# First state-space scan of a hybrid diffusion step: three task lists spread differently over the scan's steps

## The chip, the cores and the metric

The kernel runs on one core of a Trainium2 chip. A core has five engines that run their own instruction queues side by side: TensorE (PE in the rows: matrix products), VectorE (DVE: elementwise work), ScalarE (ACT: copies and activations), GpSimd (POOL, hardly used here) and SyncE (SP), whose queue issues most of the DMA transfers between HBM and the core's memory. Each queue is worked in order: an instruction that waits holds up all that stand behind it on its engine. The metric is the device time of one execution in microseconds (us), lower is better; the median of several runs is compared.

## What is computed

One inference step of a four-layer backbone on 128 context and 256 latent tokens, width 1024. Layers 0 and 3 are bidirectional diagonal state-space (S5) mixers, layer 1 pools, layer 2 is latent attention. Cut to what matters for layer 0:

```python
sh, sc, g = split(silu(cond) @ ada_w[layer] + ada_b[layer], 3)     # "conditioning", for every layer
h = rmsnorm(x) * (1 + sc) + sh
u, z = split(h @ w_in, 2)                                           # 2048 columns each
for dirn in (0, 1):                                                 # forward and backward
    bu = einsum('blgc,gpc->blgp', u_grouped, b_bar)
    states = scan(s[t] = lam_bar * s[t-1] + bu[t])                  # complex, diagonal
    y = y + real(einsum('blgp,gcp->blgc', states, c_mat))
y = gelu(y);  y = y * sigmoid(y @ glu_w + glu_b)
x = x + g * ((y * silu(z)) @ w_out)
```

The conditioning products depend on the conditioning vectors and the weights alone, so those of layers 1 to 3 can be computed at any time before their layer.

## The kernel before

The 2048 channels of the first S5 layer are worked in four **batches** of 512. The scan takes four tokens at a time, so a batch has 63 dependent **steps**; each step is three VectorE operations in a row (`Pr` products, `R` sum, `E` add, written by the helper in line 51), all on one state tile `E`. There are two `E` tiles, taken in turn, and two sets of `Pr` and `R`, so two batches can be under way at once. In steps 0 to 31 the operations are twice as wide as in 32 to 62.

`S5Body.run` (line 1231 on) makes one table of tasks for each batch `b`: at which step which piece of other work is written into the program. `rec` then writes the tasks and the steps one after the other. The pieces are:

- `u(b)`: the u columns of batch `b`, 24 products of 512 columns (line 213 on PE, four 512 KB weight loads into the `raw` ring of four buffers), and three transposing copies on DVE (line 1084) into `U`, of which there are three (names U_608, U_609, U_610; batch 3 uses the first again). They accumulate in three of the four `acc` banks.
- `win(b, qq)`: the scan's input for a quarter batch: weights prepared on DVE (tiles `w`), transposed on PE (line 910), 32 small products (line 1122), copied into `E` by ACT (line 1125). All four quarters must be in `E` before step 1 of that batch can end.
- `mats(q)`: the output matrices of one quarter (DVE tiles `P`, `t`, PE line 938, and a round trip through HBM: `Td<-Tt`, `Md<-Td`, then tile `M`). `P` has four buffers.
- `z(q)`: eight products of the gate path (line 204 on PE, one 512 KB load in the same `raw` ring, one `acc` bank, a SiLU on ACT, a store).
- `fill`: one **unit** of conditioning (line 97 to 99): two loads `adw` of 512 KB and, for each, four products of 256 columns into `adps`. These loads have two buffers (`araw`). Four units make a group, which ends with `adarow` on DVE and, for a gate, a store `gd` on the SP queue. `fill` without an argument writes four units, `fill(1)` one. 40 units fall into this scan.
- `glu.early_y` and `glu.early_prod` (batch 3 only): first parts of the following gated unit (lines 829 to 831).

After each batch `out(b, qq)` writes the outputs of its quarters: copies `Eq` of the state on ACT or DVE, then 16 products of line 1212 and four of line 1208 on PE, alternating between the banks `tp` and `ad`, a GELU and a store. For quarters 2 and 3 the matrix `M` is fetched only there. The second S5 layer has a `run` of its own and is not touched.

The order in which the program text writes the work is not the order on the engines: a list scheduler at build time goes through all instructions by the text's order as priority, with its own idea of times and of free buffers, and puts out one fixed order for each engine. So a piece of low priority whose inputs are ready is pulled ahead into gaps that the scheduler foresees. In the words below a **leg** is the stretch on PE from the first product of line 1212 of one batch to that of the next.

Of the kernel before, what the change touches and what calls it, by code (L numbers as in the profile page):

```python
# [1031 lines left out]
class S5Body:  # L1032
# [198 lines left out]
    def run(self, h, fill, glu):  # L1231
        self.h = h

        self.Es = [p.tile([128, 99, 64], F32, name="E", tag="e") for p in (self.eps[0], self.e1)]
        self.Ps, self.Ms = {}, {}
        self.u(0)
        for qq in range(4):
            self.win(0, qq)
        zs = list(range(16))
        for b in range(4):  # L1240
            tasks = {}
            at = lambda i, f, *a: tasks.setdefault(i, []).append(lambda: f(*a))
            if b < 3:
                at(4, self.u, b + 1)
            for qq in range(4):
                if b < 3:
                    at(8 + 14 * qq, self.win, b + 1, qq)
                at(6 + 14 * qq, self.mats, 4 * b + qq)
            for k in range((3, 4, 3, 6)[b]):
                at(62, self.z, zs.pop(0))  # L1250
            if fill:
                for k in range((4, 3, 2, 1)[b]):
                    at(45, fill)
            if b == 3:
                for q in range(8):
                    at(min(62, 30 + 6 * q), glu.early_y, self.wq, q)
                for q in zs:
                    at(62, self.z, q)
                for q in range(2):
                    at(62, glu.early_prod, q)  # L1260
            self.rec(b, tasks)
            for qq in range(4):
                q = 4 * b + qq
                self.out(b, qq)
                if b == 3:
                    for k in range(2, 6):
                        if (0, 1, 2, 3, 3, 3)[k] == qq:
                            glu.early_prod(k)
                if qq < 2:
                    self.Ms[q + 2] = self.m_mat(q + 2)  # L1270
        self.nc.sync.dma_start(self.A["o_s5"][self.j], self.fin.rearrange("p q g r -> p (q g r)"))
# [262 lines left out]
```

## Time and profile before

| | |
|---|---|
| median of three runs | 1808.92 us (1808.36 to 1813.42) |
| the profiled execution | 1803.79 us, its span 1802.0 us |
| busy over the span: PE, DVE, ACT | 95%, 70%, 50% |
| first S5 scan, from step 0 of batch 0 to the last output product | 90.9 to 483.3 us |
| busy in 88 to 486 us (398 us): PE, DVE, ACT | 383.1, 314.4, 195.1 us |
| granted TensorE clock, mean | 0.98 of full speed |

The rows shown further on have the start of an instruction or of a piece of the chain first, then its length, then engine, line and tiles. A PE product of 32-bit data is recorded twice in this trace, except in lines 910, 111 and 829 to 831, so x16 in line 204 are eight products. A bracket at a row's end gives the idle time of the engine just before it and what ended it. The "chain" is the sequence of work that ended last, followed back from the end.

### The profile page before, as it was taken

To read this page: it belongs to the slowest core of one execution; us is meant where nothing else is said; L and a number is where in the kernel's file an instruction comes from. 1 tells how busy PE (TensorE), PEld (TensorE's weight loads), DVE (VectorE), ACT (ScalarE), POOL (GpSimd) and SP (SyncE) were. 2 spreads that over 40 slices of the span, in tenths; PEclk is the share of its full clock that TensorE was granted. 3 is DMA by queue.
4 is the path that set the end of the run, shared out by engine and by line. 5 is a ranking of instruction groups with operands and counts; after the bars stand their busy time and mean duration, and the time that the engine had idled before them with its cause. 6 is when DMAs were issued, how large, how long until landed. Compare 5 with 4: busy or idle time off the path is not lost.

```text
span 1802.0 us, 29493 instructions
## 1 busy us (share of the span) xinstructions
PE 1706.7 (95%) x10928; PEld 1322.9 (73%) x10928; DVE 1252.6 (70%) x3149; ACT 898.9 (50%) x1588; POOL 5.4 (0%) x16
## 2 busy tenths in 40 slices
PE   4999999998999998999998999999899999899998
PEld 1464464654899877999887886567678878689986
DVE  7698786788476668888867747763439978746435
ACT  2653275625454456655546655542354554634332
POOL 0000000000000000000000000000000000000000
PEclk8999999999999999999999999999999999999999
DMA  8347756665587564555664566732567764666552
GB/s 317 94 120 236 235 178 211 192 196 158 176 246 238 184 207 134 178 160 178 187 201 130 180 212 227 242 108 88 182 219 229 228 191 135 196 205 211 173 165 73
DMA packets 174831, 334.30 MB, mean 186 GB/s; under 512 B 78528, under 2 KB 101856, under 8 KB 174688
## 3 DMA queue, kind: packets, MB, share of 16 engines
q1 hardware_dynamic: 165728, 319.84, 57.1%
q10 hardware_dynamic: 8960, 12.59, 2.1%
q8 instruction: 86, 1.41, 0.3%
q14 instruction: 57, 0.47, 0.1%
HBM read 279.54 MB, written 52.82 MB: 184 GB/s over the span
## 4 chain that ended last, share of the span: by engine, by line
PE 80%; DVE 8%; DMA 6%; ACT 4%; issue 2%; SPq 0%; ACTq 0%; DVEq 0%
PE acc L175 7%; PE acc L176 7%; PE acc L177 7%; PE sp L1122 5%; PE acc L829 4%; PE acc L830 4%; PE acc L831 4%; PE acc L159 4%; PE acc L161 4%; PE acc L160 4%; PE acc L213 4%; PE acc L204 3%; DMA adw<-in_ada_w 3%; PE ad L1212 3%; PE tp L1212 3%; PE adps L99 2%
## 5 line engine op out<-in xcount | busy, mean ns | idle before, releaser
L51 DVE TENSOR_TENSOR wlo<-raw,whi 128x1024 fp32r<-128x1024 f32 (+2 forms) x234 | 281.0, 1203 | 242.2 <-ACT whi L138 221.4
L138 ACT CAST whi<-raw 128x1024 fp32r<-128x1024 f32 x246 | 257.6, 1050 | 325.1 <-PE acc L177 131.6
L51 DVE TENSOR_TENSOR Pr<-E,Tb 128x256 f32<-128x256 f32 (+1 forms) x504 | 172.8, 352 | 8.8 <-ACT E L1131 2.8
L159 PE MATMUL acc<-hh,whi 128*128 128x384 f32 x512 | 176.6, 345 | 0.3 <-ACT whi L138 0.2
L161 PE MATMUL acc<-hh,wlo 128*128 128x384 f32 x512 | 173.6, 339 | 0.5 <-DVE wlo L51 0.5
L160 PE MATMUL acc<-hl,whi 128*128 128x384 f32 x512 | 173.8, 339 | 0.0
L829 PE MATMUL acc<-y,whi 128*128 128x384 f32 x448 | 151.6, 343 | 5.4 <-ACT y L146 3.3
L175 PE MATMUL acc<-whi,ph 128*128 128x512 f32 x384 | 153.0, 398 | 0.0
L831 PE MATMUL acc<-y,wlo 128*128 128x384 f32 x448 | 151.3, 339 | 1.0 <-DVE wlo L51 1.0
L830 PE MATMUL acc<-y,whi 128*128 128x384 f32 x448 | 151.7, 340 | 0.2 <-DVE y L51 0.2
L176 PE MATMUL acc<-wlo,ph 128*128 128x512 f32 x384 | 151.6, 395 | 0.0
L177 PE MATMUL acc<-whi,pl 128*128 128x512 f32 x384 | 151.6, 395 | 0.0
L51 DVE TENSOR_TENSOR E<-R,E 128x128 f32<-128x128 f32 (+1 forms) x504 | 121.9, 252 | 28.1 <-ACT E L1125 21.8
L51 DVE TENSOR_TENSOR R<-Pr 128x128 f32<-128x128 f32 (+1 forms) x504 | 122.6, 253 | 5.8
L159 PEld LDWEIGHTS acc<-hh,whi 128*128 128x128 f32 x512 | 96.5, 189 | 5.5 <-issue 2.3
L161 PEld LDWEIGHTS acc<-hh,wlo 128*128 128x128 f32 x512 | 96.4, 188 | 3.0 <-DVE wlo L51 1.5
L204 PE MATMUL acc<-h,raw 128*128 128x384 f32 x256 | 98.0, 513 | 0.0
L160 PEld LDWEIGHTS acc<-hl,whi 128*128 128x128 f32 x512 | 96.5, 188 | 1.0 <-issue 0.3
L99 PE MATMUL adps<-adw,scond 128*32 128x256 f32 x768 | 71.7, 428 | 25.6 <-DMA adw<-in_ada_w 24.3
L213 PE MATMUL acc<-raw,h 128*128 128x512 f32 x192 | 95.0, 613 | 0.0
L829 PEld LDWEIGHTS acc<-y,whi 128*128 128x128 f32 x448 | 83.9, 188 | 9.6 <-ACT y L146 4.7
L830 PEld LDWEIGHTS acc<-y,whi 128*128 128x128 f32 x448 | 84.2, 188 | 2.4 <-DVE y L51 0.9
(285 smaller groups left out, 3210.2 us busy)
## 6 DMA issues: line engine op xcount, KB each, us to landing
adw<-in_ada_w SPq DMA_DIRECT2D x96, 512.0 KB
raw<-in_s_glu SPq DMA_DIRECT2D x64, 512.0 KB
raw<-in_s_wu SPq DMA_DIRECT2D x48, 512.0 KB
raw<-in_s_wz SPq DMA_DIRECT2D x40, 512.0 KB
raw<-in_s_wo SPq DMA_DIRECT2D x32, 512.0 KB
yq<-yd SPq DMA_DIRECT2D x64, 192.0 KB
lod<-wlo SPq DMA_DIRECT2D x24, 512.0 KB
wlo<-lod SPq DMA_DIRECT2D x24, 512.0 KB
```

What stands on the lines that cost most here:

```text
L51: return self.nc.vector.tensor_tensor(out=out, in0=a, in1=b, op=op)
L138: nc.scalar.copy(out=hi, in_=raw)
L159: nc.tensor.matmul(ps, h, xh[:, kk, :ncol], start=i == 0, stop=False)
L160: nc.tensor.matmul(ps, h, xl[:, kk, :ncol], start=False, stop=False)
L161: nc.tensor.matmul(ps, l, xh[:, kk, :ncol], start=False, stop=i == n - 1)
L175: nc.tensor.matmul(ps, xh[:, kk, xs], h, start=kk == 0, stop=False)
L176: nc.tensor.matmul(ps, xh[:, kk, xs], l, start=False, stop=False)
L177: nc.tensor.matmul(ps, xl[:, kk, xs], h, start=False, stop=kk == 2 * nu - 1)
L213: self.nc.tensor.matmul(ps, x[:, kk, T * 128:(T + 1) * 128], w[:, k * 512:(k + 1) * 512], start=kk == 0, stop=kk == 7)
L829: self.nc.tensor.matmul(ps, h, y[:, 0, k], start=u == 0 and k == 0, stop=False)
L830: self.nc.tensor.matmul(ps, h, y[:, 1, k], start=False, stop=False)
L831: self.nc.tensor.matmul(ps, l, y[:, 0, k], start=False, stop=u == 1 and k == 7)
```

## The change

Only the task table of `S5Body.run` changes. In batch 0 `u(1)` is written at step 2 instead of 4. `u(2)` and `u(3)` are written at step 50 of batches 0 and 1 (two batches ahead) instead of at step 4 of batches 1 and 2. The quarters of `win` come every 11 steps from step 12 instead of every 14 from step 8, those of `mats` every 13 from step 10 instead of every 14 from step 6. Of the sixteen `z`, none, five, five and six stand in batches 0 to 3 instead of three, four, three and six, spread over steps (34, 41, ... 62, and 8, 17, ... 53 in batch 3) instead of all at step 62. The 40 units of conditioning are written one at a time, at steps 3, 9, ... 57 of every batch, instead of in blocks at step 45: 16, 12, 8 and 4 units.

```diff
-            if b < 3:
-                at(4, self.u, b + 1)
+            if b == 0:
+                at(2, self.u, 1)
             for qq in range(4):
+                at(10 + 13 * qq, self.mats, 4 * b + qq)
                 if b < 3:
-                    at(8 + 14 * qq, self.win, b + 1, qq)
-                at(6 + 14 * qq, self.mats, 4 * b + qq)
-            for k in range((3, 4, 3, 6)[b]):
-                at(62, self.z, zs.pop(0))
+                    at(12 + 11 * qq, self.win, b + 1, qq)
+            for k in range((0, 5, 5, 6)[b]):
+                at(34 + 7 * k if b < 3 else 8 + 9 * k, self.z, zs.pop(0))
+            if b < 2:
+                at(50, self.u, b + 2)
             if fill:
-                for k in range((4, 3, 2, 1)[b]):
-                    at(45, fill)
+                for k in range(10):
+                    at(3 + 6 * k, fill, 1)
```

What that makes of the engines' orders, at the three places that count. **Place A**, PE just ahead of the outputs of batch 0 (line 213 is u, 204 is z, 99 is conditioning, 1212 and 1208 are outputs). Before:

```order
L204 MATMUL acc<-h,raw 128x384 x4
L99 MATMUL adps<-adw,scond 32x256 x4
L204 MATMUL acc<-h,raw 128x384
L99 MATMUL adps<-adw,scond 32x256 x4
L204 MATMUL acc<-h,raw 128x384 x4
L99 MATMUL adps<-adw,scond 32x256 x4
L204 MATMUL acc<-h,raw 128x384 x2
L99 MATMUL adps<-adw,scond 32x256 x4
L204 MATMUL acc<-h,raw 128x384 x3
L1212 MATMUL tp<-Eq,P 64x96 x4
```

After:

```order
L99 MATMUL adps<-adw,scond 32x256 x4
L204 MATMUL acc<-h,raw 128x384 x3
L99 MATMUL adps<-adw,scond 32x256 x4
L204 MATMUL acc<-h,raw 128x384 x2
L1208 MATMUL ad<-U_608,M 128x96
L204 MATMUL acc<-h,raw 128x384 x2
L213 MATMUL acc<-raw,h 128x512 x8
L1212 MATMUL tp<-Eq,P 64x96 x4
```

The last eight products ahead of the outputs now belong to u(3), a third of it. From the end of u(1) to here PE has 96 conditioning products instead of 120, 24 of z instead of 38 and 32 of u instead of 24.

**Place B**, PE at the outputs of batch 1. Before:

```order
L1212 MATMUL tp<-Eq,P 64x96 x4
L213 MATMUL acc<-raw,h 128x512
L99 MATMUL adps<-adw,scond 32x256 x4
L213 MATMUL acc<-raw,h 128x512
L99 MATMUL adps<-adw,scond 32x256 x4
L213 MATMUL acc<-raw,h 128x512 x3
L99 MATMUL adps<-adw,scond 32x256 x4
L1208 MATMUL tp<-U_609,M 128x96
L213 MATMUL acc<-raw,h 128x512
```

After:

```order
L204 MATMUL acc<-h,raw 128x384 x5
L1208 MATMUL tp<-U_609,M 128x96
L1212 MATMUL tp<-Eq,P 64x96 x4
L1208 MATMUL tp<-U_609,M 128x96
L1212 MATMUL tp<-Eq,P 64x96 x4
L1208 MATMUL tp<-U_609,M 128x96
L1212 MATMUL tp<-Eq,P 64x96 x4
```

The products of u(3) and 12 loads' worth of conditioning stood among the outputs of batch 1; after, u(3) is done ahead of them and only 11 products of z stand among them.

**Place C**, the outputs of batch 3, on PE. Before:

```order
L1208 MATMUL tp<-U_608,M 128x96
L99 MATMUL adps<-adw,scond 32x256 x4
L1212 MATMUL tp<-Eq,P 64x96 x4
L1208 MATMUL tp<-U_608,M 128x96
L1212 MATMUL tp<-Eq,P 64x96 x4
```

After:

```order
L99 MATMUL adps<-adw,scond 32x256 x8
L111 MATMUL adt<-ident,adarow 128x128 x2
L1212 MATMUL tp<-Eq,P 64x96 x4
L1208 MATMUL tp<-U_608,M 128x96
L1212 MATMUL tp<-Eq,P 64x96 x4
L1208 MATMUL tp<-U_608,M 128x96
L1212 MATMUL tp<-Eq,P 64x96 x3
L99 MATMUL adps<-adw,scond 32x256 x4
L1212 MATMUL tp<-Eq,P 64x96
L1208 MATMUL tp<-U_608,M 128x96
L1212 MATMUL tp<-Eq,P 64x96 x4
L99 MATMUL adps<-adw,scond 32x256 x12
```

The SP queue there, after:

```order
L97 DMA adw<-in_ada_w 128x1024
L815 DMA yq<-yd_120 128x4x96 x2
L954 DMA Md<-Td_607 32x4x64
L107 DMA gd_119<-adarow 2x256 x4
L954 DMA Md<-Td_607 32x4x64 x3
L136 DMA raw<-in_s_glu 128x1024 x2
```

The whole last group of conditioning (32 products, eight loads) now stands behind the first output product of batch 3, where before all of it stood ahead. In both programs its store `gd` stands on the SP queue ahead of the last three parts of `Md`, the matrix of the third output quarter, and of the next weights of the gated unit.

## Rows read from the trace of the kernel before

**Rows 1.** PE timeline: the legs' first rows, the last output row.

```profile
117.69 0.99 PE L938 MATMUL sp<-Tz,Bp 128*32 128x224 f32 x16
...
212.80 0.87 PE L1212 MATMUL tp<-Eq,P 128*64 128x96 f32 x8
...
281.30 0.33 PE L1212 MATMUL tp<-Eq,P 128*64 128x96 f32 x1
...
399.77 0.94 PE L1212 MATMUL tp<-Eq,P 128*64 128x96 f32 x8 [0.20 <-ACT Eq L1188]
...
450.27 0.88 PE L1212 MATMUL tp<-Eq,P 128*64 128x96 f32 x8 [1.03 <-ACT Eq L1188]
...
482.39 0.92 PE L1212 MATMUL ad<-Eq,P 128*64 128x96 f32 x8
```

**Rows 2.** The chain in order of time: start us, us, what; PE undisturbed.

```profile
99.95 3.02 PE sp L1122 x64
102.97 14.79 PE acc L213 x34
117.76 0.92 PE sp L938 x16
...
224.80 5.19 PE acc L204 x16
...
243.09 1.00 PE adps L99 x16
...
402.31 0.80 PE tp L1212 x8
403.11 0.39 PE tp L1208 x2
```

**Rows 3.** Waits in 88 to 486 us: us in total, times, longest.

```profile
PEld adps L99 <- DMA adw<-in_ada_w: 23.6, 27, 2.4
...
DVE adarow L51 <- PE adps L99: 14.5, 9, 4.0
...
PE adps L99 <- DMA adw<-in_ada_w: 7.4, 12, 2.0
```

**Rows 4.** DVE timeline: first step, then last steps of batches 0 to 3.

```profile
90.93 0.42 DVE L51 TENSOR_TENSOR Pr<-E,Tb 128x256 f32<-128x256 f32 x1
...
206.07 0.27 DVE L51 TENSOR_TENSOR Pr<-E,Tb 128x128 f32<-128x128 f32 x1
...
207.38 0.29 DVE L51 TENSOR_TENSOR Pr<-E,Tb 128x128 f32<-128x128 f32 x1
...
208.24 0.29 DVE L51 TENSOR_TENSOR Pr<-E,Tb 128x128 f32<-128x128 f32 x1
...
270.85 0.28 DVE L51 TENSOR_TENSOR Pr<-E,Tb 128x128 f32<-128x128 f32 x1
...
282.17 0.29 DVE L51 TENSOR_TENSOR E<-R,E 128x128 f32<-128x128 f32 x1 [4.80 <-ACT E L1125]
...
395.59 0.27 DVE L51 TENSOR_TENSOR Pr<-E,Tb 128x128 f32<-128x128 f32 x1
...
446.31 0.29 DVE L51 TENSOR_TENSOR Pr<-E,Tb 128x128 f32<-128x128 f32 x1
```

**Rows 5.** The chain: conditioning loads and one fetch of M, issue to landing.

```profile
186.22 4.53 DMA adw<-in_ada_w
...
412.96 4.40 DMA Md<-Td
...
424.59 5.55 DMA adw<-in_ada_w
```

**Rows 6.** Busy us: PE, PEld, DVE, ACT, POOL; clock, DMA, GB/s; sum 88 to 486.

```profile
150.00:207.00 57.00, 53.89 (x318) 22.84 (x319) 52.01 (x234) 5.51 (x15) 0.00 (x0) 1.00 0.81 256
...
432.00:436.00 4.00, 4.00 (x14) 1.73 (x13) 3.61 (x15) 3.95 (x7) 0.00 (x0) 0.50 0.97 275
...
sum 398.00, PE 383.08 PEld 219.83 DVE 314.40 ACT 195.10 POOL 1.89; mean PE 27.36 PEld 15.70 DVE 22.46 ACT 13.94 POOL 0.14
```

## The prediction

> **What bounds the kernel now.** I read the trace from the outside in. The page shows a busy PE all through the span, so the question is what the scan, about 400 us of it, waits for. The scan's time is read on PE, leg by leg, because the legs follow one another on that queue without a break: in the timeline the reader is to take the first output product of each batch [rows 1]. From the end of u(1) the legs last 212.80 - 117.69 = 95.1, then 68.5, 118.5, 50.5 and, to the end of the last row, 33.0 us: 365.6 together.
>
> How much of that is work follows from what one product costs when nothing holds it up [rows 2]: u 14.79/17 = 0.87 us, z 5.19/8 = 0.65, conditioning 1.00/8 = 0.125, scan input (line 1122) 3.02/32 = 0.094, line 938 0.92/8 = 0.115, line 1212 0.80/4 = 0.20, line 1208 0.39. Multiplied with the products that the order of the program before has in each leg, the five legs hold 81, 62, 106, 39 and 32 us of work, 320 in all. (First leg: 38 z = 24.7, 24 u = 20.9, 120 conditioning = 15.0, 128 scan input = 12.0, small ones 9.) So PE waits 46 of 366 us: 14, 7, 12, 12 and 1. The table of waits says for what: PE and its weight loads wait 23.6 + 7.4 = 31 us for conditioning loads (the two columns may overlap), and DVE another 14.5 for conditioning products, with the scan's steps queued behind [rows 3].
>
> DVE is the other chain. A late step that stands alone takes 208.24 - 207.38 = 0.86 us [rows 4]; when steps of two batches alternate, the distances between the operations shrink. Summing DVE's order with the distances in the timeline, waits left out, the first step of batch 0 to the last of it takes 103 us, and from last step to last step 42, 97 and 42. The trace has its last steps at 206.1, 270.9, 395.6 and 446.3 us, the first at 90.9 [rows 4], so DVE waited 12, 23, 27 and 9 us. Both queues are thus some 85% full and hold each other up in turn; from 150 to 207 us DVE is busy for 52 of 57 us and the transfers for 0.81 of it [rows 6].
>
> **The change, part by part.** It adds and removes no instruction of weight; it moves them, and the scheduler has moved them once more. So the sum is the new order's work on each leg, plus the waits that I expect there. By the order after, the legs hold 76, 72, 89, 47 and 36 us, again 320.
>
> *First leg* (place A). PE has 5 us less, and 24 conditioning loads instead of 30, over some 87 us: 3.6 us each, where a load takes 4.5 to 5.6 us and two are under way [rows 5], 2.3 to 2.8 us each. DVE's sum to the last step of batch 0 hardly moves (102 us), so its waits decide: 12 us before, of which some 5 for conditioning. I take 7 (bounds 2 and 12). The last step then comes at 90.9 + 102 + 7 = 199.7 instead of 206.1, and the outputs as much earlier: leg 88.5 us instead of 95.1.
>
> *Second leg.* Here it costs: PE has 10 us more, chiefly the 16 other products of u(3) (13.9 us) and more z. DVE gets through its 46 us before that, so PE sets the end. Its waits were 7 us, with conditioning in a row at the end of it; the last scan input of batch 2 came so late that DVE stood 4.8 us at 282.17, and 11 us lie between its last step at 270.85 and that row [rows 4]. With 16 loads over 76 us I take 4 (0 to 8): 76 us instead of 68.5. New is a wait on DVE: the last two transposing copies of u(3) stand on its queue after step 2 of batch 2, and behind them all steps of that batch. PE is through with u(3) one conditioning load and 16 z products (some 13 us) ahead of the outputs of batch 1, at about 268 us; DVE, with 46 us of work and some 14 of waits behind 199.7, could be there at 260. It loses 8 us of an advance, not of the leg.
>
> *Third leg* (place B). What was paid is back: PE has 18 us less, since u(3) and most of the conditioning are out of the outputs, which frees `P` buffers earlier for DVE. DVE needs 95 us without waits, 91 of them from those copies on. From 268 that is 359; with some 13 us for `P` buffers and conditioning (before: 27 in all) the last step comes at 372. On PE 89 + 6 (2 to 12) gives 95 us instead of 118.5; both agree.
>
> *Fourth leg.* It lasts as long as batch 3's remaining steps on DVE: 42 us before, 46 after (three more steps, two more `P`, one `adarow`, all counted), plus 9 of waits as before (4 to 12): 55 instead of 50.5. PE's 47 fit under it. Before, the clock fell to 0.50 of full speed, the lower level (1.2 GHz), in 432 to 436 us after waits for loads [rows 6]; that may not recur, which I count in the bound.
>
> *Fifth leg* (place C). The eight loads of the last group now stand behind the batch's first output. Two buffers and up to 5.5 us per pair give four rounds, 22 us from the leg's start. Then come `adarow`, the store `gd` and behind it on SP the fetch of `M`, 4.4 us [rows 5] and some 3 around it: the third output quarter starts at 29. With two quarters (5 us each) and the products between (4 us) behind it the leg ends at 44 instead of 33. The floor is 36, the work alone; if each load had to wait for the one ahead, eight rounds, it would be 66.
>
> The trace has 4.5 and 5.6 us for such a load [rows 5]. The Trainium skill, DMA: Bandwidth & Descriptors, section Anatomy of one DMA, fits 2.0 us plus the bytes at 436 GB/s (for transfers issued by GpSimd; these are issued by SP), so an estimate of 3.2 us for 512 KB; by it the four rounds take 13 us, this leg ends near its floor and the sum would be 1793. The rows are slower than the page, with other transfers beside them, and they decide.
>
> *Sum*: 88.5 + 76 + 95 + 55 + 44 = 358.5 instead of 365.6, rounded 7 us less; with the clock's two and the doubt about the second leg's 4 I say 8. The gated unit behind the scan keeps its work, and later stages their order but for small shifts, counted at nothing, since PE is full there; without that cover a late `yq` or weight load of a few us would show. The sum is made against the profiled execution, 1803.8 us, of which 1802.0 is the span. The three runs' median is 1808.9; the gain is taken off that: **1801 us**.
>
> **Rivals.**
>
> *Slower: the tail eats the middle.* The conditioning that was ahead of the last output is now behind it, with `gd` and `M` queued after it. For it: place C, and that the SP queue there also holds `yq` loads, which wait for their buffers. If the eight loads go one by one, the leg lasts 66 us, 22 more than I count: 1823. It decides from 52 us on, when the 8 are gone. Against it: two buffers, and loads in pairs in the trace.
>
> *No change: the waits stay.* If PE's waits are not the loads but the mutual holding up of two in-order queues, each leg keeps its wait (second 7, third 12): 9 us back, 1809 to 1810. The new copies of u(3) on DVE speak for it. That the change does not do what it says belongs here: three z are still pulled ahead of batch 0's outputs.
>
> *Faster: the tail is free.* If a pair of loads takes the shorter 4.5 us [rows 5] and the output and gated products between them (some 15 us up to the last load) fill most of the rounds, the last leg is 36: 8 us more, 1793.
>
> *PE is the bound throughout.* PE is busy for 383 of 398 us in the scan [rows 6]; if that were work, nothing over 15 us could ever be had. The products' prices say 320 of 366. The Trainium skill, Perfetto Trace Analysis, section Identifying the Most-Contended Engine, holds that matmul busy time is no good measure here; the trace agrees, by those numbers. So this one gets no chance of its own.
>
> **How the numbers follow.** My forecast has a chance of 0.37, faster still 0.17, no change 0.25, slower 0.21. A measurement of this kernel tells about 0.3%, 5.4 us, from no change: faster than 1803.5 is then 0.53 (the forecast's case but for one point, and the faster one), within 0.26, slower 0.21. The range reaches from just under the faster case to halfway into the slower one, 1790 to 1816: it leaves out perhaps 0.07 below and 0.12 above.
>
> **What would show it.** Right: the outputs of batch 1 start within 5 us of 281, those of batch 2 before 385, the last ones before 440; PE's waits for conditioning loads fall under 25 us and gather behind the last outputs' start; the last leg is 40 to 50 us. Wrong in the middle: batch 2's outputs after 392, with DVE waiting for line 213 at line 1084. Wrong at the end: a last leg over 52 us, or under 38.

## The result, and the profile after

The changed kernel is slower: 1826.66 us against 1809.2 us, medians of four runs each taken side by side. The ratio of their means is 1.0088 with a 95% interval of 1.0065 to 1.0111, some 16 us. The profiled execution took 1822.4 us, its span is 1820.6 (1802.0 before). Forecast were 1801 us and a range that ended at 1816.

The legs first, on PE's timeline of the changed kernel (start, us, engine, line, operation, count, and in brackets what PE waited for): the row behind u(1), the first output product of each batch, one row between the halves of batch 0's outputs, the last output row.

```profile
117.80 1.07 PE L99 MATMUL adps<-adw,scond 128*32 128x256 f32 x16
...
208.20 0.91 PE L1212 MATMUL tp<-Eq,P 128*64 128x96 f32 x8 [3.48 <-ACT Eq L1188]
...
221.36 0.91 PE L1212 MATMUL tp<-Eq,P 128*64 128x96 f32 x8 [3.04 <-ACT Eq L1188]
...
290.39 0.92 PE L1212 MATMUL tp<-Eq,P 128*64 128x96 f32 x8
...
392.49 0.88 PE L1212 MATMUL tp<-Eq,P 128*64 128x96 f32 x8
...
451.03 0.91 PE L1212 MATMUL tp<-Eq,P 128*64 128x96 f32 x8
...
500.34 0.92 PE L1212 MATMUL ad<-Eq,P 128*64 128x96 f32 x8
```

Against [rows 1] the batches' outputs start at 208, 290, 392 and 451 instead of 213, 281, 400 and 450 us, and the last output row ends at 501.3 instead of 483.3. So the scan is 18 us longer, which is the whole difference of the two spans:

| leg | before | forecast | after |
|---|---|---|---|
| 1, to the outputs of batch 0 | 95.1 | 88.5 | 90.4 |
| 2, to batch 1 | 68.5 | 76 | 82.2 |
| 3, to batch 2 | 118.5 | 95 | 102.1 |
| 4, to batch 3 | 50.5 | 55 | 58.5 |
| 5, to the end | 33.0 | 44 | 50.2 |
| sum | 365.6 | 358.5 | 383.5 |

Every leg is longer than forecast, by 2, 6, 7, 3.5 and 6 us. The work is the same 320 us; the waits are 63 instead of the 46 of before and the 38 of the forecast. The table of waits (88 to 505 us: total, times, longest) says for what:

```profile
PEld adps L99 <- DMA adw<-in_ada_w: 33.1, 27, 3.5
...
PE adps L99 <- DMA adw<-in_ada_w: 18.5, 15, 2.9
...
DVE adarow L51 <- PE adps L99: 14.4, 8, 4.8
...
PE tp L1212 <- ACT Eq L1188: 6.5, 2, 3.5
```

The two rows for loads were 23.6 and 7.4 [rows 3]: the waits that the change was forecast to shrink below 25 us have grown from 31 to 52 (the two rows may overlap). DVE, on the other hand, is where it was. Its steps that end batches 2 and 3 come at 385.38 and 447.43 (395.59 and 446.31 in [rows 4]):

```profile
385.38 0.29 DVE L51 TENSOR_TENSOR Pr<-E,Tb 128x128 f32<-128x128 f32 x1
...
447.43 0.29 DVE L51 TENSOR_TENSOR Pr<-E,Tb 128x128 f32<-128x128 f32 x1
```

Ten of the hoped-for microseconds were there at the end of batch 2, and gone at the end of batch 3. The 17 us of loss lie between DVE's last step and the last output row: 36 us before, 53 after.

### The profile page after: what moved, and what is told of

It is laid out like the page before. It is cut to its first block, busy times and chain, and to the rows that moved or that the text cites. A ratio compares the mean times of both kernels' runs of the same rounds, so it can differ in the third digit from the quotient of the medians.

```text
span 1820.6 us, 29497 instructions
## 1 busy us (share of the span) xinstructions
PE 1710.6 (94%) x10928; PEld 1329.6 (73%) x10928; DVE 1256.0 (69%) x3149; ACT 899.1 (49%) x1587; POOL 5.4 (0%) x16
## 4 chain that ended last, share of the span: by engine, by line
PE 79%; DVE 8%; DMA 7%; ACT 4%; issue 2%; SPq 0%; ACTq 0%; DVEq 0%
PE acc L175 6%; PE acc L176 6%; PE acc L177 6%; PE sp L1122 5%; DMA adw<-in_ada_w 4%; PE acc L829 4%; PE acc L830 4%; PE acc L831 4%; PE acc L159 4%; PE acc L161 4%; PE acc L160 4%; PE acc L213 4%; PE ad L1212 3%; PE acc L204 3%; PE tp L1212 3%; PE adps L99 2%
```

## A third chain: the loads

The prediction weighed two queues, PE's and DVE's. The traces of the two kernels, read side by side, show a third. On the SP queue of the changed kernel, most conditioning loads go out in pairs; here a stretch ahead of the outputs of batch 2 (start, us from the first issue to the second's end):

```profile
365.23 2.39 SPq L97 DMA_DIRECT2D adw<-in_ada_w  x2
...
370.70 2.44 SPq L97 DMA_DIRECT2D adw<-in_ada_w  x2
...
376.78 2.32 SPq L97 DMA_DIRECT2D adw<-in_ada_w  x2
...
382.12 2.38 SPq L97 DMA_DIRECT2D adw<-in_ada_w  x2
...
387.52 1.77 SPq L97 DMA_DIRECT2D adw<-in_ada_w  x2
```

In this stretch a pair starts every 5.3 to 6.1 us. Over all 80 loads of the scan, in both kernels, half of the loads are read within 5.4 us of their issue, and half of the buffers are reissued within 0.06 us of being read. So the two buffers are nearly always on their way: the loads are a chain with a pace of its own, 3.0 us per load, whether or not PE has gaps to hide them in. It pauses only where the order has no conditioning product for a while and both buffers lie full. PE's conditioning rows around the longest pauses (only those of 7 us or more are counted), first of the kernel before, then of the changed one:

```profile
216.60 0.64 PE L99 MATMUL adps<-adw,scond 128*32 128x256 f32 x8
...
243.02 1.07 PE L99 MATMUL adps<-adw,scond 128*32 128x256 f32 x16
...
382.14 0.64 PE L99 MATMUL adps<-adw,scond 128*32 128x256 f32 x8 [0.24 <-DMA adw<-in_ada_w]
...
423.92 1.05 PE L99 MATMUL adps<-adw,scond 128*32 128x256 f32 x16
...
448.60 0.64 PE L99 MATMUL adps<-adw,scond 128*32 128x256 f32 x8
```

```profile
194.21 0.64 PE L99 MATMUL adps<-adw,scond 128*32 128x256 f32 x8
...
234.53 1.05 PE L99 MATMUL adps<-adw,scond 128*32 128x256 f32 x10
...
284.69 0.64 PE L99 MATMUL adps<-adw,scond 128*32 128x256 f32 x8
...
317.53 0.42 PE L99 MATMUL adps<-adw,scond 128*32 128x256 f32 x3
...
388.27 0.64 PE L99 MATMUL adps<-adw,scond 128*32 128x256 f32 x8
...
423.91 1.07 PE L99 MATMUL adps<-adw,scond 128*32 128x256 f32 x16
```

Between the end of one group and the start of the next, the kernel before pauses 26, 14 (at 321 us) and 41 us, the changed one 40, 32 and 35, and twice 7 to 8 at other places: 81 us against 122. From the first to the last load's products it is 330 us before and 357 after, which leaves 249 and 235 us for 79 loads, 3.0 to 3.15 each. So 41 us more of pauses made the last load 25 us later, with the other 14 us or so won back in the pace. The last products come at 448.6 before and, in the rows of the tail, at 474.11 after:

```profile
454.93 1.08 PE L99 MATMUL adps<-adw,scond 128*32 128x256 f32 x8
...
474.11 0.64 PE L99 MATMUL adps<-adw,scond 128*32 128x256 f32 x8
474.67 0.45 PE L831 MATMUL acc<-y,wlo 128*128 128x384 f32 x1
475.29 0.46 PE L1208 MATMUL ad<-U,M 128*128 128x96 f32 x2 [0.17 <-DVE adarow L51]
...
486.46 0.46 PE L1208 MATMUL tp<-U,M 128*128 128x96 f32 x2 [2.81 <-ACT M L957]
```

The second quarter of the last outputs starts 1.2 us behind the last load's products: it stands in the one buffer of the pool `ad`, which the conditioning group (`adps`) holds until `adarow` has read it. The third follows 11 us later, behind the second and behind M.

The pauses were to be had before the run. Priced as in [rows 2], the work between two conditioning products is 25, 14 and 39 us in the order before and 31, 32 and 34 us in the order after, 20 us more (the two short pauses left out; in the trace the first is longer than its price, 40 us, as PE also waits for `Eq` in it).

## The experiments

Three theories stood against each other: L (the loads are the loss; P in the later runs: their chain with its pauses), C (cover: u and z no longer stand between the outputs of batch 0, so PE waits for Eq there and its clock falls), and D (loads cost the same wherever they are). The legs and the order tell them apart better than the time does. All ratios are to the kernel before, timed on the same chip; a **unit** is two loads, as above.

| kernel | ratio (95%) | last load's products | DVE's last step | last output row |
|---|---|---|---|---|
| before | 1 | 448.6 | 446.3 | 482.4 |
| changed | 1.0088 (1.0065 to 1.0111) | 474.1 | 447.4 | 500.3 |
| conditioning alone | 1.0144 (1.0121 to 1.0166) | 481.9 | 448.0 | 511.3 |
| u alone | 1.0059 (1.0041 to 1.0077) | 444.2 | 466.6 | 492.8 |
| z alone | 1.0072 (1.0053 to 1.0091) | 461.5 | 465.8 | 494.4 |
| win, mats alone | 1.0024 (1.0009 to 1.0038) | 452.0 | 443.0 | 485.5 |
| changed, conditioning as before | 1.0068 (1.0051 to 1.0084) | 459.4 | 460.9 | 492.5 |
| changed, z as before | 1.0068 (1.0048 to 1.0088) | 468.8 | 449.1 | 497.3 |
| changed, 12/12/12/0 units | 1.0051 (1.0033 to 1.0069) | 402.5 | 466.8 | 491.6 |
| changed, 12/12/12/4 units | 1.0059 (1.0037 to 1.0082) | 445.8 | 464.6 | 492.1 |
| changed, half the loads | 0.9914 (0.9895 to 0.9932) | 431.5 | 437.9 | 465.1 |
| before, half the loads | 0.9918 (0.9900 to 0.9937) | 417.6 | 437.9 | 466.1 |
| changed, loads among the outputs | 1.0016 (1.0007 to 1.0024) | 448.4 | 456.7 | 486.8 |
| the same, z as cover | 1.0005 (0.9989 to 1.0020) | 443.1 | 455.1 | 486.2 |
| the same, z and u as cover | 1.0060 (1.0045 to 1.0076) | 448.6 | 460.4 | 495.1 |
| before, last units among the outputs | 1.0025 (1.0013 to 1.0037) | 406.7 | 462.6 | 490.4 |
| before, last units at step 3 | 1.0037 (1.0024 to 1.0050) | 445.5 | 456.8 | 487.8 |
| before, 20 units in the scan | 1.0086 (1.0067 to 1.0105) | 333.5 | 431.4 | 470.0 |
| changed, 20 units in the scan | 1.0099 (1.0078 to 1.0121) | 335.5 | 439.2 | 470.6 |
| before, 12 units in the scan | 1.0105 (1.0084 to 1.0126) | 331.0 | 429.9 | 457.8 |

(The three columns of times are starts in us, read from one profiled execution each, which took up to 6 us more or 5 less than the median of its kernel. The two kernels with half the loads compute other values.)

**Half the loads, in both kernels.** The test of whether loads are the loss: only the first load of each pair is issued, and the products of both read it.

```diff
-                raw = self.ring.tile([128, 4, 256], F32, name="adw", tag=tag, bufs=4 if tag == "raw" else 2)
-                nc.sync.dma_start(raw, self.A["ada_w"][l, g, k])
+                raw = raw if k % 2 and not first else self.ring.tile([128, 4, 256], F32, name="adw", tag=tag, bufs=4 if tag == "raw" else 2)
+                k % 2 and not first or nc.sync.dma_start(raw, self.A["ada_w"][l, g, k])
```

> The changed kernel with half of the conditioning loads left out: of each pair of steps k, k+1 only the first tile is loaded, and both products read it (the conditioning values are therefore others; products as many as before). Its order is that of the changed kernel up to the outputs of batch 1; with fewer loads to count the scheduler puts all conditioning ahead of the last outputs. Theory L (loads): PE's idle time for loads falls from 18.5 to under 6 us, the last leg from 50 to about 25 with 20 us more work in the fourth, so 10 to 18 us less than the changed kernel, level with the kernel before or faster. Theory C (cover): the two waits for Eq at the outputs of batch 0 (3.5 and 3.0 us) and the granted clock of 0.50 behind them stay, and with them the 82 us of the second leg; if that is the whole loss, the time stays 12 us or more above the kernel before.

> The kernel before with the same half of the conditioning loads left out. Theory L: its waits for loads (7.4 us on PE, 23.6 on the weight loads) mostly go, 5 to 12 us less than before. Theory M (mutual: the queues hold each other up, whatever the loads): within 4 us of before.

With half the loads the two orders take the same time, and each is 15 us faster than the kernel before with all of them. The table's change costs 0.9% with all loads and nothing with half. The savings are larger than L expected: 31 us below the changed kernel instead of 10 to 18, and 15 below the kernel before instead of 5 to 12. The waits of the changed kernel's order with half the loads (88 to 470 us):

```profile
PE tp L1212 <- ACT Eq L1188: 7.6, 3, 4.2
PEld adps L99 <- DMA adw<-in_ada_w: 6.4, 7, 1.8
...
PE adps L99 <- DMA adw<-in_ada_w: 2.8, 5, 1.2
```

The waits for Eq are still there, longer than in the changed kernel, and with them a second leg of 81.6 us; they cost nothing in the end. Theory L holds and C falls as the cause. With half the loads the other edits gain nothing either: DVE's last step is at 437.9 in both. Fewer loads could also help by leaving room for other transfers; but in the changed kernel PE waits only 0.3 us for other transfers and DVE 2.2. (Leaving loads out also let more products of the gated unit and all conditioning come ahead of the last outputs, so this shows that loads are the loss, not yet where.)

**The four parts, each alone on the kernel before.**

```diff
-                for k in range((4, 3, 2, 1)[b]):
-                    at(45, fill)
+                for k in range(10):
+                    at(3 + 6 * k, fill, 1)
```

> The kernel before with the conditioning alone changed (one unit every six steps). 24 conditioning products, six loads, stand behind the first output of batch 3. Theory L: last leg 42 to 48 us instead of 33, PE's waits for conditioning loads above the 7.4 us of before, time 1817 to 1826. Theory C: u and z are where they were, so 1806 to 1812.

By the conditioning alone it is 1.0144, more than the whole change, and 26 us: six loads stand in the last leg, the last at

```profile
475.70 1.08 PE L99 MATMUL adps<-adw,scond 128*32 128x256 f32 x8 [3.20 <-DMA adw<-in_ada_w]
...
481.90 1.08 PE L99 MATMUL adps<-adw,scond 128*32 128x256 f32 x8
```

with the last leg at 48.8 us, where L had 42 to 48; the time too is above L's 1817 to 1826, and far above C's 1806 to 1812. (Four conditioning products take 1.08 us here and 0.64 elsewhere: the clock is at its lower level, its mean in this leg is 0.75.)

```diff
-            if b < 3:
-                at(4, self.u, b + 1)
+            if b == 0:
+                at(2, self.u, 1)
 ...
+            if b < 2:
+                at(50, self.u, b + 2)
```

> The kernel before with u alone changed (u(1) at step 2, u(2) and u(3) at step 50 of batches 0 and 1); z and conditioning as before, no conditioning behind the last outputs. Theory L: not slower than before, 1798 to 1811. Theory C: the second leg, which gets 82 us of work instead of 62, is paid in full and not won back, 1815 or more.

```diff
-            for k in range((3, 4, 3, 6)[b]):
-                at(62, self.z, zs.pop(0))
+            for k in range((0, 5, 5, 6)[b]):
+                at(34 + 7 * k if b < 3 else 8 + 9 * k, self.z, zs.pop(0))
```

> The kernel before with z alone changed (0, 5, 5, 6, spread). 12 conditioning products instead of 8 and 11 products of z stand between the outputs of batch 0; no conditioning behind the last outputs. Theory L: within 5 us of before, either way. Theory C: without z between the outputs PE waits for Eq there and the clock falls, 6 to 15 us slower than before.

```diff
+                at(10 + 13 * qq, self.mats, 4 * b + qq)
                 if b < 3:
-                    at(8 + 14 * qq, self.win, b + 1, qq)
-                at(6 + 14 * qq, self.mats, 4 * b + qq)
+                    at(12 + 11 * qq, self.win, b + 1, qq)
```

> The kernel before with the scan inputs and matrices alone at their new steps (win at 12 + 11 per quarter, mats at 10 + 13). Its order differs little from that of before: 4 conditioning products (one load) behind the first output of batch 3, legs' work 81, 62, 109, 36, 32. Theory P: 0 to 6 us slower than before. If these steps are where the changed kernel loses, 10 us or more slower.

u alone and z alone are slower by 0.6 and 0.7%, which L did not expect. The sizes are what C had, the legs are not: with u alone legs 2 and 3 together take 182.7 us (187.0 before), with z alone 187.4, and the loss is in the fourth, 74 and 71 us instead of 50.5. No load is behind the last outputs in either; DVE's last step is late, 466 instead of 446 us (with z alone the last load too, 461). For u the books close: its order has 328 us of PE work ahead of the last output instead of 320 (products of the gated unit that moved ahead of it) and 48 us of waits instead of 46, and the last row is 10 us later. win and mats alone cost 0.24%. The parts together (0.88%) are less than their sum (2.99%). A reading that fits, and that no run tests: each alone upsets the balance of the chains, and what one makes late is no later for the next.

**Taking the loads out of the tail.**

```diff
-                for k in range(10):
-                    at(3 + 6 * k, fill, 1)
+                for k in range((4, 3, 2, 1)[b]):
+                    at(45, fill)
```

> The changed kernel with the conditioning as before (blocks of 4, 3, 2, 1 calls at step 45 of each batch); u, z, win and mats stay changed. In its order no conditioning product stands behind the first output of batch 3 (the changed kernel has 32 there, eight loads). Theory L (loads: the loss is PE standing for conditioning loads that come in pairs every 5.9 us, and the last eight of them behind the last outputs): last leg about 33 us instead of 50.2, PE's idle time for loads back from 18.5 to under 10 us, time 1803 to 1812. Theory C (cover: the loss is that u and z no longer stand between the outputs of batches 0 and 1, so PE idles for the Eq copies and its granted clock falls to 0.50): the waits of 3.5 and 3.0 us at the outputs of batch 0 and the 0.84 clock stay, and the time stays at 1820 or above.

```diff
-                for k in range(10):
-                    at(3 + 6 * k, fill, 1)
+                for k in range(12 if b < 3 else 0):
+                    at(3 + 5 * k, fill, 1)
```

> The changed kernel with the 36 conditioning units emitted in the first three batches (12 each, one every five steps) and none in batch 3. No conditioning product is behind the first output of batch 3; 16 instead of 32 lie between the outputs of batches 2 and 3. Theory L: the last leg falls under 30 us and the time to 1800 to 1812. Theory C: the legs of batches 0 and 1 stay 90 and 82 us, time 1815 to 1825.

```diff
-                for k in range(10):
-                    at(3 + 6 * k, fill, 1)
+                for k in range(12 if b < 3 else 4):
+                    at(3 + (5 if b < 3 else 6) * k, fill, 1)
```

> The changed kernel with its 40 units as 12, 12, 12 and 4 (one every five steps, in the last batch every six), so that one group is left for batch 3 as in the kernel before and none of it stands behind the last outputs. Theory L with the tail as the main place: last leg 25 to 30 us, 8 to 16 us less than the changed kernel, level with before. Rival (loads cost the same in the middle): the fourth leg grows by what the last one loses, within 5 us of the changed kernel.

(The kernel with no units in batch 3 has its last eight loads behind the scan.) The last legs are 28, 22 and 26 us instead of 50, as L had it, but the times are only 0.2 to 0.4% less than the changed kernel's, with intervals that overlap its own. That is well short of L, and for the first two nearer to what C had for the time: the fourth leg grew from 58.5 to 67, 78 and 76 us, with DVE's last step back at 461 to 467. Most of what the tail loses comes up there, as the rival in the third expectation has it. The remedy for the tail alone is worth some 4 to 7 us of 16, if that.

```diff
-            for k in range((0, 5, 5, 6)[b]):
-                at(34 + 7 * k if b < 3 else 8 + 9 * k, self.z, zs.pop(0))
+            for k in range((3, 4, 3, 6)[b]):
+                at(62, self.z, zs.pop(0))
```

> The changed kernel with z as before (3, 4, 3, 6 at step 62). Nine products of u(3) now stand between the outputs of batch 0, where the changed kernel has nothing; 20 conditioning products (five loads) are behind the first output of batch 3 instead of 32. Theory C: no wait of 3 us for Eq in the outputs of batch 0 and a clock of 1.00 in 204 to 228 us, second leg 78 us of work and little more; 5 to 8 us less than the changed kernel. Theory L: the last leg shrinks by three loads (8 us); legs 2 and 3 stay; also 5 to 8 us less. The legs tell the two apart, not the time.

Five loads behind the last outputs, last leg 46.3 us; the clock is 1.00 at the outputs of batch 0 and the second leg is 85 us all the same, where C had 78 and little more. The time, 1.0068, is not clearly below the changed kernel's; both theories had 5 to 8 us less. The cover moved nothing that counts.

**Fewer units in the scan.** If loads are the loss, why not elsewhere? (20 units: calls 2, 2, 1, 0; the changed kernel 8, 8, 4, 0; 12 units: 1, 1, 1, 0.)

```diff
-                for k in range((4, 3, 2, 1)[b]):
+                for k in range((2, 2, 1, 0)[b]):
```

> The kernel before with 20 instead of 40 conditioning units in the scan (calls 2, 2, 1, 0 at step 45), the others in later stages. Theory L: scan 328 us instead of 366, of which 10 go to later stages as products; total 8 to 20 us less than before, within 4 us of the changed kernel with the same number. Rival D: within 5 us of before.

> The changed kernel with 20 instead of 40 conditioning units emitted in the scan (8, 8, 4, 0, one every six steps); the other 20 follow in later stages, nothing is left out. 40 loads instead of 80 in the scan, none behind the last outputs. Theory L (the loss is loads whose pairs take 5.9 us and which are placed where PE has nothing else): the scan's legs fall to about 330 us (302 of work, 28 of waits as with half the loads); later stages take 10 us of conditioning products and, if their loads are hidden there, nothing more, so 12 to 25 us less than the changed kernel, and less than the kernel before. Rival D (deferred: the loads cost the same wherever they are): scan shorter, later stages longer by as much, within 6 us of the changed kernel.

> The kernel before with 12 instead of 40 conditioning units in the scan (calls 1, 1, 1, 0). Theory L: another 3 to 8 us less than with 20 units, if later stages hide 28 units as well; Rival D: no gain over before; in between, later stages are full from some number on and the 12 are slower than the 20.

The scan ends 12 us earlier with 20 units and 25 with 12, and the whole is slower by 0.9 to 1.05%: the later stages lose 28 to 44 us. Of these, 20 to 28 are PE's work for the 160 or 224 products that moved with the loads (0.125 us each, [rows 2]; the expectation's 10 us was half of it). L's forecasts of 8 to 25 us less failed. Rival D was right for the changed kernel (1.0099 for 1.0088) and too mild for the kernel before. Where the other 8 to 16 us go stays open; at the numbers tried, these loads are cheaper in the scan than behind it.

**Shorter pauses.** The test of the chain: two units of each of the first three batches are emitted among its outputs, batch 3 has four units, and the rest of the change stays.

```diff
-                for k in range(10):
+                for k in range(10 if b < 3 else 4):
                     at(3 + 6 * k, fill, 1)
 ...
-                self.out(b, qq)
+                self.out(b, qq); fill and b < 3 and fill(qq % 2)
```

> The changed kernel with conditioning among the outputs again: 10 units in the steps of batches 0 to 2, one more behind the second and fourth output quarter of each, 4 in batch 3. In its order the stretches of PE work without conditioning sum to 69 us from the outputs of batch 0 on (changed kernel 97, kernel before 77). Theory P (the loads are a chain of their own, 3.0 us per load as long as the order asks for them, and stand with both buffers full where it doesn't): the last conditioning product comes 20 to 28 us earlier than 474.7, at 447 to 455, none behind the last outputs, last leg 25 to 28 us instead of 50; the time falls by 4 to 12 us, no further, since DVE's last step is then late as in the kernels with 12 units a batch (465). If only the number of loads counted, the last product would stay at about 475.

PE's rows of the last load, of the first output of batch 3 and of the last output:

```profile
448.39 0.64 PE L99 MATMUL adps<-adw,scond 128*32 128x256 f32 x8 [0.64 <-DMA adw<-in_ada_w]
...
460.32 0.99 PE L1212 MATMUL tp<-Eq,P 128*64 128x96 f32 x8
...
486.84 0.92 PE L1212 MATMUL ad<-Eq,P 128*64 128x96 f32 x8
```

The pauses are 94 us in the trace instead of 122, the last load's products come at 448, where P put them (447 to 455), and the last leg is 27.4 us. Of 0.88% loss 0.16 are left, some 13 us back where P had 4 to 12, with u, z, win and mats still at their new steps. But an early last load alone does not do it: the kernel with 12/12/12/4 units has as many units in each batch, pauses of 92 us and its last load at 445.8, and is 0.59% slower. What differs is DVE's last step, 464.6 instead of 456.7 us.

```diff
-                for k in range((4, 3, 2, 1)[b]):
+                for k in range((4, 3, 2, 0)[b]):
 ...
-                self.out(b, qq)
+                self.out(b, qq); fill and b == 2 and fill(1)
```

> The kernel before with the last four units moved from batch 3 into the outputs of batch 2, where it has 38 us of PE work without conditioning. Theory P: the last conditioning product comes at 415 to 430 us instead of 449. If the chain of loads sets the end of the scan in the kernel before, the time falls by 5 to 15 us; if DVE's chain or the gated unit's early products set it as well, it stays within 5 us of before, or is up to 10 us slower since 8 us more of these products stand ahead of the last outputs.

The same on the kernel before brings the last load to 407, earlier than expected, and 0.25% of loss: there DVE's chain, at 446, was no earlier than the loads, and it gets later (463). In the kernel before the two chains end within 2.3 us of each other.

```diff
-                    at(45, fill)
+                    at(45 if b < 3 else 3, fill)
```

> The kernel before with the last batch's four units at step 3 instead of 45. Same stretches without conditioning, so by theory P the last product stays near 449 us and the time within 3 us; 6 us of the gated unit's products come ahead of the last outputs, and if such products delay the last outputs the time rises by 3 to 8 us.

0.37% slower at the same pauses, as expected of products of the gated unit that come ahead of the last outputs: DVE's last step is 10 us later.

**Cover for the outputs of batch 0**, on top of the shorter pauses: z as 2, 4, 4, 6, in the first kernel with batch 0's at step 62, in the second spread, with u(2) and u(3) at step 62.

```diff
-            for k in range((0, 5, 5, 6)[b]):
-                at(34 + 7 * k if b < 3 else 8 + 9 * k, self.z, zs.pop(0))
+            for k in range((2, 4, 4, 6)[b]):
+                at(62 if b == 0 else 34 + 7 * k if b < 3 else 8 + 9 * k, self.z, zs.pop(0))
```

> The kernel with conditioning among the outputs, with z as 2, 4, 4, 6 and those of batch 0 at its last step: seven products of u(3) now stand between the outputs of batch 0, where there was nothing. Work ahead of the last output 322 us, as in the kernel before (320). Theory C for the rest: no wait of 3 us for Eq and a granted clock of 1.00 there, second leg 80 us or less instead of 89, 3 to 9 us less than the kernel it is made from, so 0 to 7 us less than before. If the waits there cost nothing in the end, since DVE's chain sets it: within 3 us of the kernel it is made from.

> The same with z as 2, 4, 4, 6 spread and u(2), u(3) at step 62 instead of 50: twelve products of z between the outputs of batch 0, as in the kernel before (11 and 8 of conditioning). Same expectations: by theory C 3 to 9 us less than the kernel it is made from; else within 3 us of it.

In the first, PE does not wait there, its clock is 1.00 throughout these outputs, and the second leg falls from 89.1 to 79.9 us, just as C had it. The time is that of the kernel before, 1.0005 with an interval across 1; the step from 1.0016 is within what these runs can tell. Legs 1 and 3 took back 3.5 and 3.8 us, the last one 1.2: the 9 us were not on the path. In the second the second leg stays at 90 us, and it is 0.6% slower. No kernel here that issues all its loads beats the kernel before.

## Why the prediction was wrong

*What held.* That the work is the same and only waits differ; that legs 2, 4 and 5 lengthen and legs 1 and 3 shorten; the first leg (90.4 for 88.5). The eight loads behind the last outputs end 23 us into the leg, forecast was 22, but that is partly luck: the first pair was issued at 445.83 us, 5 us ahead of the leg, and the other three rounds took 5.0 to 5.9 us each. The slower rival was this tail, and its direction came true. Its 1823 us is near the measured time by luck: it charged the tail alone with 66 us, while the leg of 50.2 us is under its 52, the loads did not all go one by one, and 19 of the 25 us by which the sum was short lie in the other legs. The signs of being right failed: the outputs of batches 1 to 3 start at 290, 392 and 451 us (forecast within 5 of 281, before 385 and before 440); only the last leg was near its 40 to 50.

*The step that failed* is the one that set the loads against the time within each leg ("24 conditioning loads ... over some 87 us: 3.6 us each", "16 loads over 76 us"). On average they fitted, so PE's waits were sized down, to 4 us in leg 2 and 6 in leg 3. But the loads are a chain through all legs, and time in which the order asks for no load is lost to it: the pauses grew from 81 to 122 us, the last load came 25 us later, PE's waits for loads rose from 31 to 52 us, and with half of the loads the whole loss is gone. In place B, conditioning that leaves the outputs of batch 1 was counted as 18 us less work on PE and earlier `P` buffers. The buffers brought 2 us (DVE's waits for them fell from 16.1 to 14.1 us); the price was a pause that grew from 14 to 32 us. (A slip without weight: 90.9 + 102 + 7 is 199.9, not 199.7.)

*Mis-sized terms.* Second leg, 82.2 for 76: not the loads, for which PE never stands there, but 3.0 us of waiting for Eq and the lower clock behind it; by the half-load and cover runs this one would have been free. Third leg, 102.1 for 95: PE idles 5.4 us for loads, and DVE waits for steps queued behind them; with half the loads this leg is 86.2 at 82 of work, so the rest of it was sized about right. Fourth, 58.5 for 55: 4.3 us for loads. Fifth, 50.2 for 44: I let the second output quarter run beside the loads; it waits for the group's buffer, so the third started 35 us into the leg instead of 29. And the clock, counted as 2 us to gain: its means in the five legs are 0.99, 0.92, 0.98, 0.96 and 0.88 instead of 1.00, 1.00, 1.00, 0.93 and 1.00. An estimate from these means and the legs' lengths is 18 us of full clock missing instead of 3.5, 6 of them in the last leg, where a wait of 2.47 us for a load (to 462.66) is followed by 0.57 in 463 to 467 us. So part of what the waits cost comes by the clock; no run changed it by itself.

*The rivals.* "The tail is free" is refuted: 50.2 us for its 36. "The waits stay" came out on the other side: they grew by 17. "Wrong in the middle", by DVE waiting for u(3) at line 1084, is refuted as a mechanism: that wait is 0.2 us in the trace, though batch 2's outputs came at 392.5. The estimate of 13 us for the four rounds, by the Trainium skill's figure (DMA: Bandwidth & Descriptors, section Anatomy of one DMA), is not what the trace shows: from the first load's products of the tail to the last it is 19 us, three rounds.

*What stays open.* How the late loads become time in full. In every kernel, but the one before, that has all 80 loads ahead of the last outputs, DVE's last step moves to 455 to 467 us. The traces say what stands ahead of it: from the first step to the last DVE is busy for 291 us in the kernel before and for 298 to 307 in these nine, 7 to 16 more, while its idle time there (65 us before) differs by -3 to 8. The work is splits of the gated unit (5 to 11 us instead of 1.7) and some 5 us for the last matrices `P`, `t` and `Tt`, which follow the last step in the kernel before. The same holds for the two kernels with equal units per batch: 299.0 and 306.6 us busy, 7.6 of the 8 us between their last steps, 2.3 of them the gated unit's. How much of this is lost at the end, where the work would come anyway, no run shows: none took it away by itself. What the runs do show: the last output row starts 26 to 35 us behind the later of the two, last load or last step, in every kernel with all loads in the scan, and the kernel before has the two nearly together.

## What to carry to other kernels

A stream of loads through few buffers is a chain like an engine's queue: count its loads times its pace, add the stretches of the order in which nothing reads it, and compare where it ends, before asking leg by leg whether its loads are hidden. Moving its consumers away from a stretch makes that stretch shorter and the stream later. In this kernel, whose chains end within 2.3 us of each other, none of the moves tried here was a gain. Look too at what the scheduler pulls ahead into the time that such a move frees. And waits that vanish in one place (the 9 us at the outputs of batch 0) are a gain only if nothing else was going to end there anyway.

## What the hardware showed

PE's clock. Stretches of the changed kernel's outputs of batch 0 (us; then busy time and count of PE, PE's weight loads, DVE, ACT, POOL; granted clock, transfers' share, GB/s), behind the waits of 3.48 us (to 208.20) and 3.04 us (to 221.36):

```profile
204.00:208.00 4.00, 0.72 (x2) 0.00 (x0) 3.69 (x16) 2.80 (x2) 0.00 (x0) 0.89 0.00 0
208.00:212.00 4.00, 3.80 (x28) 2.87 (x28) 3.52 (x15) 3.45 (x5) 0.00 (x0) 0.50 0.01 2
212.00:216.00 4.00, 4.00 (x34) 3.00 (x34) 2.83 (x7) 2.68 (x4) 0.00 (x0) 0.76 0.00 0
...
228.00:232.00 4.00, 4.00 (x40) 2.58 (x40) 2.26 (x7) 0.28 (x2) 0.00 (x0) 1.00 0.15 49
```

The granted clock is 0.50, its lower level (1.2 GHz), right behind the wait, and back at 1.00 within some 8 us; an output group with its product of line 1208 takes 1.51 us there (208.20 to 209.71) and 1.20 at full clock. A wait of 1.55 us, to 180.61 us, was followed by no such fall: the granted clock is 1.00 from 180 to 188 us. With seven products of u(3) between these outputs (the first of the kernels with cover) the stretch reads:

```profile
208.00:212.00 4.00, 4.00 (x25) 2.27 (x23) 3.52 (x15) 3.95 (x4) 0.00 (x0) 1.00 0.26 86
```

The other surprise is how steady the loads' pace is: 2.9 to 3.3 us per load outside pauses of 7 us or more, on the mean of the scan, in every kernel with all 80 of them in it, however differently these orders arrange what runs beside.
